# State-space phase and feed-forward opening of a hybrid layer: 108 named additions to VectorE, in a newly written order

## The chip, the cores and the metric

One core of a Trainium2 chip. The metric is the device time of one execution in microseconds (us). Engines: PE (TensorE, matrix products), DVE (VectorE), ACT (ScalarE), POOL (GpSimd) and SP, which here issues DMA transfers.

## The reference, cut to what matters

```python
xn = _rms_norm(h, pre_mix_norm); proj = xn @ w_in           # 2048 x 1024 tokens
y_ssd  = _ssd_mixer(...)      # state space: 16 chunks of 128 tokens, a running state, gate, norm
y_rwkv = _rwkv7_mixer(...)    # recurrent mixer
mix = concat([y_ssd, y_rwkv]) @ w_out
h  = h + _rms_norm(mix, post_mix_norm);  hn = _rms_norm(h, pre_ffn_norm)
u  = _causal_dwconv(hn @ ffn_w_up) ;  gate, val = split(u, 2)
y  = h + _rms_norm((silu(gate) * val) @ ffn_w_down, post_ffn_norm)
```

## The kernel before, in words

Three phases follow each other: `phase_R` (recurrent mixer, blocks R0 to R15), `phase_S` (state space, chunks C0 to C15 with shared work P0 to P7 for pairs of chunks, output projection and first residual), `phase_F` (feed-forward).

**Phase S.** A chunk n has these steps, each a list of small sub-steps that are numbered from 0. `z` is the gate projection; `decay` and `begin` make the decay matrix `Dt` and the inputs `Xdt`, `yt`; `off` (L1729) multiplies the old state into `of` and adds it to `yt` (sub-step 2, L1746); `y` (L1748) adds the products `py` (L1756, L1779), gates, squares and scales; `state` (L1783) first multiplies the old state `ST` by the chunk's decay (sub-step 0, L1794), then adds the new products (L1796); `o` is the output projection; `post` (L1849) does both norms, adds the input row (`m` plus `xi`, L1877), splits the result into two f16 halves (`hl` and, by L1862, the lower half in `xi`), turns both with DMA transposes into `tu` (L1867) and adds the turned halves into `hT` (`joined`, L1871: post.0/14 and post.1/4), which goes to DRAM (`HN`).

**Phase F** multiplies by a Strassen-like scheme of seven products. Blocks of `hn` (`hs`, loaded from `HN`) and of the weights (`us` from `w_up`, `r` from `w_down`) are added and subtracted (`ht`, `ut`, `rt`; L1946, L2098), then each is split into two f16 parts: ACT writes the upper part, DVE (L1976, L1978, L2329) the lower. The parts `w` are one buffer for each of the seven products; a part is stored to DRAM (`UW`) and read by the products `u` (L2125). DVE gathers the products in `C` (L2147), a convolution follows (L2182), then `p`, and its factors `fa` and `ft` (L1976, L2235).

**What sets the order.** From the end of phase R to the first 140 operations of phase F (the steps named E.0 and on) every step is built once in the order `TAIL`; then each engine's instructions are chained in the order in which their steps stand in the table `ORDER` (2325 names). So each engine, SP's DMA queue included, takes its work strictly in that order. After the table the planner `Program.run` orders phase F.

In phase F's entry and in `off`, `state` and `post` the two-operand additions without a PSUM operand are on POOL (`G_`) before.

Of the kernel before, what the change touches and what calls it, by code (L numbers as in the profile page):

```python
# [336 lines left out]
R14.solve/49 R15.low.1/0 R15.d.3/2 R13.finish.0/3 R15.low.1/1 R15.low.0/4 R14.solve/50 R14.solve/51 R14.solve/52
R14.conv.7/11 R14.solve/53 R15.low.1/2 R14.solve/54 R15.low.1/3 R14.solve/55 R13.finish.0/4 R15.d.5/0 R15.low.1/4
R13.finish.1/0 R15.d.5/1 R15.d.3/3 R15.d.3/4 R15.low.1/5 R15.scan/0 R14.solve/56 R14.solve/57 R13.finish.1/1
R14.values/0 R13.finish.1/2 R15.d.5/2 R15.low.1/6 R15.low.1/7 R14.solve/58 R13.finish.1/3 R14.solve/59 R14.solve/60  # L340
R15.d.6/0 R15.d.7/0 R14.solve/61 R15.low.1/8 R15.scan/1 R14.values/3 R13.finish.1/4 R15.low.1/9 R15.scan/3 R15.norm/4
R14.solve/62 R15.d.8/0 R15.d.5/3 R15.scan/4 R15.d.5/4 R14.values/1 R15.keys/0 R15.keys/1 R15.norm/0 R14.own.0/0
R14.solve/63 R15.norm/7 R15.d.7/1 R15.d.7/2 R14.solve/64 R14.solve/65 R14.solve/66 R15.norm/1 R15.scan/2 R15.d.9/0
R15.d.10/0 R15.norm/2 R14.solve/67 R14.solve/68 R14.solve/69 R15.norm/6 R14.solve/70 R14.solve/71 R15.d.9/1 R15.norm/5
R14.solve/72 R14.solve/74 R15.norm/8 R15.norm/12 R15.d.9/2 R15.d.7/3 R15.d.7/4 R15.norm/3 R14.values/4 R13.finish.1/5
R15.d.11/0 R15.d.9/3 R15.d.9/4 R15.d.12/0 R14.values/2 R15.norm/10 R15.receptance/0 R15.norm/11 R15.norm/9
R15.gram.0/0 R14.low.0/6 R14.solve/73 R14.solve/75 R15.receptance/2 R14.turn/0 R14.solve/76 R15.d.11/1 R14.conv.5/11
R14.turn/1 R14.merge.0/0 R15.gram.1/0 R15.gram.0/1 X.left/8 R14.own.0/1 R14.merge.0/1 R14.solve/77 R14.merge.0/2
R15.gram.0/2 R14.solve/78 X.left/7 R15.receptance/1 R15.gram.1/2 R14.own.0/2 R15.transposed.0/0 R15.gram.1/1
R14.merge.1/0 R13.finish.1/6 X.wdt/0 X.wz.0/0 R14.merge.1/1 R14.merge.1/2 R14.update.0/0 R14.update.0/1 R15.d.11/2  # L350
R15.transposed.0/1 X.wdt/1 X.wz.0/1 R15.solve/1 R15.d.13/0 R15.receptance/3 R15.receptance/4 X.wz.0/2 R13.finish.1/7
R15.d.13/1 R15.solve/0 R14.state.0/2 R15.solve/8 R15.d.11/3 R15.d.11/4 X.wdt/2 R15.solve/3 R13.finish.1/8
R14.state.0/5 R15.solve/2 R15.solve/7 R15.solve/5 R15.d.13/2 R15.solve/6 R15.solve/4 R15.conv.0/0 R14.own.1/0
R14.state.0/3 R14.state.1/0 P0.load.1/0 R15.conv.1/0 R14.state.0/4 R14.state.1/1 R13.finish.1/9 X.left/3 X.wz.1/0
R14.state.0/6 R15.solve/9 R15.conv.2/0 R15.solve/10 X.left/1 X.wz.0/3 R15.transposed.0/2 R14.own.1/1 R15.d.13/3
R15.conv.1/1 X.wz.0/4 X.wdt/3 R14.own.1/2 R15.d.13/4 R15.solve/11 R15.solve/12 R15.conv.1/2 X.left/2 R15.conv.3/0
R15.conv.1/3 R15.conv.1/4 X.left/5 R15.conv.3/1 R15.conv.3/2 R15.conv.1/5 P0.load.0/0 R14.update.1/0 X.wz.2/0
R15.conv.1/6 R15.conv.3/3 R15.transposed.1/0 R15.conv.3/4 R15.conv.1/7 R15.conv.3/5 R15.solve/13 R15.solve/14
R15.conv.3/6 R14.update.1/1 R15.solve/15 R15.solve/16 R15.solve/17 R15.solve/18 R15.solve/19 R15.solve/20 R15.solve/21
R15.solve/22 R15.solve/23 R15.solve/24 R15.solve/25 R15.solve/26 R15.solve/27 R15.solve/28 R15.solve/29 R15.solve/30  # L360
R15.solve/31 R14.state.1/5 R15.conv.3/7 R14.state.1/2 X.wz.1/3 R15.conv.1/8 R14.state.1/6 R14.gate/0 R15.conv.4/0
# [5 lines left out]
X.left/6 R15.solve/48 R15.solve/49 X.wz.2/4 R15.conv.5/3 X.wz.3/0 R15.solve/50 R15.solve/51 R15.conv.7/1 C0.z.1/0
R15.values/1 R15.conv.3/11 P1.load.0/0 R15.solve/52 R15.solve/53 R15.solve/54 R15.conv.5/4 R15.values/2 R15.conv.5/5
X.wz.3/1 R15.own.0/0 R15.values/3 X.wz.3/2 X.wz.3/3 C0.z.2/0 R15.conv.5/6 R15.solve/55 X.wz.3/4 C0.z.3/0
R14.finish.1/0 R15.own.0/1 C1.z.0/0 R15.conv.7/2 P0.steps/1 R15.solve/56 R15.solve/57 R15.solve/58 R15.solve/59  # L370
R15.solve/60 C1.z.1/0 C0.z.3/1 R15.conv.7/3 R15.conv.7/4 R15.solve/61 R15.solve/62 R15.conv.5/7 R15.conv.1/11 C0.z.3/2
R15.solve/63 R15.solve/64 P0.steps/2 R15.conv.7/5 X.wo.0/0 R15.conv.7/6 P0.steps/3 R15.conv.5/8 P1.load.1/0
R15.conv.5/9 P0.steps/4 R15.conv.7/7 C1.z.2/0 R15.low.0/5 X.wo.1/0 R15.solve/65 R15.conv.7/8 C0.begin/0 P0.steps/5
P0.steps/6 R15.conv.5/10 P0.sums/0 C0.begin/3 X.wo.0/1 X.wo.0/2 R15.solve/66 R15.solve/67 P0.sums/1 P0.flip/0
P0.flip/1 R15.solve/68 R15.solve/69 R15.solve/70 R15.solve/73 X.left/11 R15.solve/72 R15.solve/71 C0.z.3/3
R15.solve/74 R15.conv.7/9 R15.conv.7/10 C1.z.3/0 X.wo.1/1 X.left/9 X.wo.2/0 C1.z.3/1 R15.conv.5/11 X.wo.1/2 P1.steps/0
R15.solve/75 R15.solve/76 P0.flip/2 R15.conv.7/11 X.wo.3/0 P1.steps/1 C2.z.0/0 C2.z.1/0 C2.z.2/0 R15.solve/77
R15.values/4 R15.turn/0 R14.finish.1/1 R14.finish.1/2 R14.finish.1/3 R14.finish.1/4 P1.steps/2 R15.solve/78
R15.own.0/2 X.left/12 C1.z.3/2 X.wo.2/1 R15.turn/1 C0.rows/0 C1.z.3/3 R15.merge.0/0 R15.merge.0/1 C0.off/0
C0.decay.0/0 R15.merge.0/2 C0.decay.0/1 R15.merge.1/0 C0.decay.0/2 C0.decay.0/3 C2.z.3/0 C0.decay.1/0 C0.decay.0/4  # L380
P1.steps/3 R14.finish.1/5 C0.begin/1 R15.merge.1/1 C0.decay.0/6 C0.decay.0/7 R15.update.0/0 C2.z.3/1 C3.z.0/0
R14.finish.1/6 C0.decay.1/1 P2.load.0/0 X.wo.3/1 R15.update.0/1 C0.decay.1/2 C0.begin/2 C0.decay.1/3 X.wo.2/2
R15.state.0/0 C2.z.3/2 R15.state.0/5 R14.finish.1/7 C1.rows/0 R14.finish.1/8 R15.state.0/1 X.wo.4/0 X.wo.3/2
C0.decay.1/4 C0.decay.1/6 R15.merge.1/2 C3.z.1/0 X.wo.5/0 R15.state.0/2 C0.decay.1/8 C0.decay.0/5 X.wo.6/0 R15.own.1/0
R15.state.0/6 C3.z.2/0 P0.sums/2 C0.off/1 R15.state.0/3 X.wo.4/1 R15.state.0/4 C0.off/2 C0.decay.1/5 C0.decay.1/7
X.wo.4/2 R15.own.1/1 R15.own.1/2 C0.y/0 R15.update.1/0 X.wo.5/1 P1.steps/4 C0.y/1 R15.update.1/1 C0.y/2 C0.keys/0
# [2304 lines left out]
```

## Time and profile before

| | |
|---|---|
| median of 3 runs | 2531.79 us (2530.23 to 2536.94) |
| the profiled execution | 2531.92 us, span of its trace 2530.1 us |
| mean granted clock of TensorE | 0.983 of full speed |
| busy over the span | PE 95%, DVE 75%, POOL 48%, ACT 47% |

How it is read: busy times add up an engine's instructions, whatever waits for them. PEclk is the granted clock: 1.00 is 2.4 GHz and 0.5 is 1.2 GHz, so 0.93 over a stretch is a mix of both. The table ORDER covers about 798 to 1376 us of the span, of which 893 to 1246 us are mostly chunks.

### The profile page before, as it was taken

How to read it: one execution, taken by the hardware profiler on the slowest of the kernel's cores; microseconds unless marked ns; L12 is line 12 of the kernel's file. 1: busy time of each engine (PE TensorE's matmuls, PEld its weight loads, DVE VectorE, ACT ScalarE, POOL GpSimd, SP SyncE). 2: the span in 40 equal slices, each digit the busy share in tenths (PEclk: the TensorE clock that was granted, in tenths of full speed). 3: DMA queues.
4: the chain of work that ended last, by engine and by line, in shares of the span. 5: the costliest groups of instructions: out<-in, count | busy, mean ns of one | idle time of the engine just before them, and what ended most of it. 6: DMA issues, size and time to landing. Idle time of an engine off the chain costs nothing. (4 is left out here: it accounts for less than half of the span.)

```text
span 2530.1 us, 53854 instructions
## 1 busy us (share of the span) xinstructions
PE 2397.2 (95%) x21207; PEld 1516.7 (60%) x21212; DVE 1893.3 (75%) x3687; ACT 1198.0 (47%) x2407; POOL 1219.6 (48%) x1237
## 2 busy tenths in 40 slices
...
PEclk8899999999999999999999999999999999999999
...
GB/s 221 69 74 69 56 79 77 67 58 78 81 63 59 189 138 148 174 171 131 183 180 174 179 133 175 171 142 170 136 142 215 168 114 97 105 104 100 87 159 108
DMA packets 344413, 319.13 MB, mean 126 GB/s; under 512 B 203232, under 2 KB 248672, under 8 KB 340832
## 3 DMA queue, kind: packets, MB, share of 16 engines
...
q8 instruction: 166, 2.72, 0.4%
...
## 5 line engine op out<-in xcount | busy, mean ns | idle before, releaser
L2125 PE MATMUL u<-b,w 128*128 128x512 f16 x3696 | 811.0, 382 | 35.9 <-ACT C L2143 10.1
L2125 PEld LDWEIGHTS <-w 128*128 128x128 f16 x3696 | 363.1, 98 | 480.2 <-issue 40.3
L618 PE MATMUL d<-xt,wr 128*128 128x129 f16 x5376 | 333.8, 224 | 19.6 <-DMA xt<-xh 14.6
L618 PEld LDWEIGHTS <-wr 128*128 128x128 f16 x5376 | 320.2, 100 | 33.7 <-issue 15.9
L2365 PE MATMUL d<-dw,fa 128*128 128x512 f16 x1512 | 332.2, 379 | 5.2 <-DMA dw<-DW 2.9
L2365 PEld LDWEIGHTS <-fa 128*128 128x128 f16 x1596 | 156.4, 98 | 204.2 <-issue 16.1
L2147 DVE TENSOR_TENSOR C<-u,C 128x512 f32<-128x512 f32 x220 | 150.7, 685 | 159.8 <-PE u L2125 154.6
L618 PE MATMUL c<-xt,wc 128*128 128x131 f16 x3072 | 195.9, 224 | 11.0 <-ACT rc L846 4.8
L618 PEld LDWEIGHTS <-wc 128*128 128x128 f16 x3072 | 182.0, 98 | 17.5 <-issue 9.9
L2378 DVE TENSOR_TENSOR acc<-d,acc 128x512 f32<-128x512 f32 x212 | 140.3, 685 | 52.7 <-PE d L2365 51.8
L1976 POOL TENSOR_TENSOR fa<-p,fa 128x512 f16<-128x512 f32 x100 | 142.2, 1436 | 41.7 <-ACT fa L1971 41.7
L1978 DVE SCALAR_TENSOR_TENSOR w<-us,w 128x512 f16<-128x512 f32 x132 | 141.0, 1079 | 19.6 <-ACT w L1971 18.5
L2182 DVE SCALAR_TENSOR_TENSOR p<-C,fpar,p 128x1024 f32<-128x1024 f32 x88 | 127.5, 1449 | 34.5 <-ACT p L2178 34.5
L870 DVE SCALAR_TENSOR_TENSOR ca<-c,cw,ca 128x128 f32<-128x128 f32 x360 | 113.7, 345 | 29.9 <-ACT ca L860 25.8
L2182 DVE SCALAR_TENSOR_TENSOR a<-C,fpar,a 128x1024 f32<-128x1024 f32 x88 | 126.5, 1438 | 8.5 <-ACT a L2178 7.2
L1042 DVE TENSOR_TENSOR tmp<-atl,xl 128x60 f32<-128x60 f32 (+24 forms) x465 | 118.5, 255 | 16.4 <-DMA atl<-ATd 4.8
L2098 POOL TENSOR_TENSOR us<-us,us 128x512 f32<-128x512 f32 x66 | 109.2, 1657 | 44.6 <-DVE w L1978 23.5
L2143 ACT ACTIVATE C<-u 128x512 f32<-128x512 f32 x88 | 52.1, 592 | 162.1 <-PE u L2125 131.6
L1971 ACT ACTIVATE fa<-p 128x512 f16<-128x512 f32 x110 | 65.5, 623 | 125.2 <-DVE p L2195 113.4
L1971 ACT ACTIVATE w<-us 128x512 f16<-128x512 f32 x132 | 80.1, 623 | 91.5 <-POOL us L2098 29.3
L1048 DVE TENSOR_TENSOR xl<-xl,tmp 128x60 f32<-128x60 f32 (+24 forms) x465 | 112.3, 242 | 14.5
L2188 POOL COPY fcarry<-C 128x2 f32<-128x2 f32 x88 | 38.1, 434 | 161.6 <-DVE C L2147 161.6
...
## 6 DMA issues: line engine op xcount, KB each, us to landing
...
```

What stands on the lines that cost most here:

```text
L618: nc.tensor.matmul(ps, w[:, a, kt, :], xt[:, b, kt, cols], start=n == 0, stop=n == 3 * KT - 1)
L870: V.scalar_tensor_tensor(out=acc[:, q], in0=m["rc", e][:, q, k:k + 128], scalar=cw[:, e + q, k:k + 1], in1=acc[:, q], op0=ALU.mult, op1=AL ...
L1042: chain.tensor_tensor(out=self.tmp[:, :k, :n], in0=self.atl[:, j, j + 1:32].unsqueeze(1).to_broadcast([P, k, n]), in1=self.xl[:, :k, j:j + ...
L1048: chain.tensor_tensor(out=self.xl[:, :k, j + 1:32], in0=self.xl[:, :k, j + 1:32], in1=self.tmp[:, :k, :n], op=ALU.add)
L1971: S.activation(h, src, AF.Copy, **({} if scale is None else {"scale": scale}))
L1976: {"V": V, "G": G_}[engine].tensor_tensor(out=l, in0=src, in1=h, op=ALU.subtract)
L1978: V.scalar_tensor_tensor(out=l, in0=src, scalar=scale, in1=h, op0=ALU.mult, op1=ALU.subtract)
L2125: nc.tensor.matmul(bk[at], self.w[i][:, u, k, :], self.half.b[i][:, k, v, :], start=start and n == 0, stop=n == 11, skip_group_check=True)
L2147: op("V", .61, lambda: V.tensor_tensor(out=part(j, x), in0=bk[at], in1=part(*a), op=ALU.add), (("u", 4 * s + at), (*(c0, c1)[a[0]], a[1])) ...
L2182: V.scalar_tensor_tensor(out=o[j], in0=C[j][:, 2 - d:1026 - d], scalar=cw(g, 2 - d), in1=o[j], op0=ALU.mult, op1=ALU.add)
L2365: nc.tensor.matmul(bk[s, t], pairs[m].a[i][:, u, t * P:t * P + P], pairs[m].w[n][0][:, v, :], start=new and m == 0 and u == v == 0, stop=m ...
L2378: V.tensor_tensor(out=acc[j][:, t], in0=bk[s, t], in1=acc[j][:, t], op=ALU.add)
```

## The change

A set `SWAP` of 108 step names is added. While a step is built, `Steps.now` holds its name, and `either(G_, V)` gives DVE for a step in `SWAP`, POOL for every other. The additions of `off`, `state`, `post` and of phase F's `add`, `sub`, `plus` go through `either`. The table `ORDER` is written anew for all engines, with the same 2325 names.

```diff
+def either(pool, vector):
+    return vector if Steps.now in SWAP else pool
...
 def note(name, step):
...
+    Steps.now = name
     tc = Steps.made["tc"]
     n = len(traced(tc))
     step()
     Steps.made[name] = list(traced(tc)[n:])
+    Steps.now = None
...
 ORDER = """
-R14.conv.7/9 R13.state.1/3 R15.d.0/0 R13.state.1/4 R14.conv.7/10 R13.state.1/6 R13.finish.0/0 R14.d.13/1 R15.d.1/0
...
+SWAP = frozenset("""
+C0.off/2 C0.state/0 C1.off/2 C1.state/0 C2.off/2 C0.post.0/14 C2.state/0 C3.off/2 C1.post.0/14 C1.post.1/4 C3.state/0
...
+""".split())
...
-                products, scaled, lambda: G_.tensor_tensor(out=self.yt, in0=self.yt, in1=self.t, op=ALU.add)]
+                products, scaled, lambda: either(G_, V).tensor_tensor(out=self.yt, in0=self.yt, in1=self.t, op=ALU.add)]
...
-                lambda: G_.tensor_tensor(
+                lambda: either(G_, V).tensor_tensor(
                     out=s1, in0=s0, in1=self.aend.unsqueeze(2).to_broadcast([P, 8, 64]), op=ALU.mult),
...
-                G_.tensor_tensor(out=self.hT, in0=self.tu[:, 0], in1=self.tu[:, 1], op=ALU.add)
+                either(G_, V).tensor_tensor(out=self.hT, in0=self.tu[:, 0], in1=self.tu[:, 1], op=ALU.add)
...
         def sub(out_, a, b):
-            G_.tensor_tensor(out=out_, in0=a, in1=b, op=ALU.subtract)
+            either(G_, V).tensor_tensor(out=out_, in0=a, in1=b, op=ALU.subtract)
...
-                    op("G", 1.25, lambda: G_.tensor_tensor(out=st[o], in0=st[a], in1=st[b], op=alu), (n[a], n[b]), (n[o],))
+                    op("G", 1.25, lambda: either(G_, V).tensor_tensor(out=st[o], in0=st[a], in1=st[b], op=alu), (n[a], n[b]), (n[o],))
```

The same edit is made in `add`, in the plus of `factors` (L2235) and in the addition of L1877, of which no step is in `SWAP`.

Counted in the built programs, 103 instructions go from POOL to DVE: 16 of `off` (L1746), 13 of `state` (L1794), 27 of `post` (L1871), 29 of L1946, 15 of L2098 and 3 of L2235. The other five names in `SWAP` (E.306, E.310, E.313, E.317, E.319) are the lower halves of `fa`, whose function has no `either`: they stay on POOL. In the new order 35 of the 103 stand before the products `py` of chunk 10, 11 more before those of chunk 12, and 57 behind them. Lines of the changed kernel are 17 higher from `phase_R` on (L1746 is L1763 there).

**Place 1: chunk 13 joins its state while chunk 11 is finished.** POOL before; `hT_110` is chunk 11's first joined half, `ST0` the state, `sgr` a norm's factor, `hs` and `ht` blocks of the feed-forward input.

```order
L1746 TENSOR_TENSOR yt_13_20555<-yt_13_20555,of_13_20570 128x512
L1608 TENSOR_SCALAR pnv_20683<-ssh_11_20681 128x1
L1612 TENSOR_TENSOR pnr_20685<-pnv_20683,mhalf_s_17704 128x1
L1794 TENSOR_TENSOR ST0_17025<-ST1_17026,aend_13_20584 128x512
L1946 TENSOR_TENSOR hs00310_21480<-hs00310_21480,hs00300_21476 128x512
L1871 TENSOR_TENSOR hT_110_20693<-tu_110_20690 128x512
L1608 TENSOR_SCALAR sgv_20719<-sgs_13_20715 128x2
L1946 TENSOR_TENSOR ht003_21487<-hs00311_21482,hs00310_21480 128x512
L1612 TENSOR_TENSOR sgr_20721<-sgv_20719,mhalf_s_17704 128x2
```

DVE with the change, the same place; the first row makes the lower half that the transposes turn for chunk 11's second half.

```order
L1879 TENSOR_TENSOR xi_11_20367<-xi_11_20367,hl_11_20672 128x512
L1993 TENSOR_TENSOR b2_0_21429<-hs00210_21460,b2_0_21429 128x512
L1993 TENSOR_TENSOR b0_0_21420<-hs00300_21476,b0_0_21420 128x512
L1658 SCALAR_TENSOR_TENSOR sz_13_20612<-th_13_20614,sz_13_20612 128x512
L1888 TENSOR_TENSOR hT_110_20693<-tu_110_20690 128x512
L1811 TENSOR_TENSOR ST0_17025<-ST1_17026,aend_13_20584 128x512
L1796 TENSOR_TENSOR yt_13_20555<-py_13_20704,yt_13_20555 128x512
L1813 TENSOR_TENSOR ST0_17025<-pst_13_20750,ST0_17025 128x512
L1797 TENSOR_TENSOR yt_13_20555<-yt_13_20555,sz_13_20612 128x512
```

The joined half, which waits for a DMA, and the state's multiply now stand in DVE's queue, ahead of chunk 13's `yt` and state.

**Place 2: the third weight block of the opening.** POOL before: the differences `ut`, `us` of weight block 3 between the down-projection's `r` and the factors `fa` of block pair 0.

```order
L1946 TENSOR_TENSOR ut_0_3_22119<-us_0_300_22078,us_0_310_22053 128x512
L2098 TENSOR_TENSOR us_0_310_22053<-us_0_310_22053,us_0_311_22102 128x512
L2098 TENSOR_TENSOR us_0_300_22078<-us_0_310_22053,us_0_300_22078 128x512
L1946 TENSOR_TENSOR r_0_0_21791<-rt_0_0_21792,r_0_0_21791 128x512
L1946 TENSOR_TENSOR r_0_1_22056<-r_0_1_22056 128x512
L1946 TENSOR_TENSOR rt_0_1_22057<-r_0_1_22056 128x512
L1976 TENSOR_TENSOR fa4_0_0_21960<-p_0_1_21933,fa4_0_0_21960 128x512
L2235 TENSOR_TENSOR ft_0_0_21949<-p_0_1_21933,p_0_0_21710 128x512
```

DVE with the change, the same weight block.

```order
L1963 TENSOR_TENSOR ut_0_3_22119<-us_0_300_22078,us_0_310_22053 128x512
L2164 TENSOR_TENSOR C_0_21_22074<-u_0_21_22060,C_0_20_22073 128x512
L2164 TENSOR_TENSOR C_0_21_22074<-u_0_22_22081,C_0_21_22074 128x512
L1879 TENSOR_TENSOR xi_15_21180<-xi_15_21180,hl_15_21269 128x512
L1995 SCALAR_TENSOR_TENSOR w5_0_2_21884<-us_0_201_21857,w5_0_2_21884 128x512
L2199 SCALAR_TENSOR_TENSOR a_0_1_21939<-C_0_11_21808,fpar_21405,a_0_1_21939 128x1024
L2115 TENSOR_TENSOR us_0_310_22053<-us_0_310_22053,us_0_311_22102 128x512
L2212 TENSOR_TENSOR p_0_1_21933<-p_0_1_21933,a_0_1_21939 128x1024
L2115 TENSOR_TENSOR us_0_300_22078<-us_0_310_22053,us_0_300_22078 128x512
L2252 TENSOR_TENSOR p_0_0_21710<-p_0_0_21710,p_0_1_21933 128x512
```

The weight differences now alternate on DVE with the gathering of products, the convolution and the splits; POOL keeps the `fa` halves and the small copies.

## Rows read from the trace of the kernel before

**Rows 1.** The page: busy time, share and instructions of engines, and the granted clock in 40 slices of the span.

```profile
PE 2397.2 (95%) x21207; PEld 1516.7 (60%) x21212; DVE 1893.3 (75%) x3687; ACT 1198.0 (47%) x2407; POOL 1219.6 (48%) x1237
...
PEclk8899999999999999999999999999999999999999
```

**Rows 2.** Busy time of each engine in five windows that cover the table ORDER (from:to and length, busy us and instructions of each engine; then the granted clock, the DMA share and GB/s).

```profile
core 0: us, PE busy (x) PEld busy (x) DVE busy (x) ACT busy (x) POOL busy (x), PEclk, DMA share, GB/s
798.00:893.00 95.00, 91.81 (x1313) 74.40 (x1310) 69.09 (x190) 55.38 (x124) 50.15 (x96) 1.00 0.46 143
893.00:1112.00 219.00, 215.37 (x1299) 125.14 (x1302) 142.34 (x305) 97.83 (x277) 95.75 (x107) 0.99 0.53 145
1112.00:1168.00 56.00, 52.50 (x301) 29.50 (x300) 38.15 (x74) 26.09 (x68) 31.00 (x31) 1.00 0.80 214
1168.00:1246.00 78.00, 63.62 (x304) 34.10 (x305) 59.24 (x92) 37.19 (x98) 46.40 (x45) 0.89 0.46 127
1246.00:1374.00 128.00, 104.21 (x460) 45.89 (x460) 100.46 (x98) 56.59 (x94) 100.36 (x80) 0.93 0.64 199
```

**Rows 3.** What PE waited for, 1168 to 1374 us (total, times, longest).

```profile
PE u L2125 <- ACT w L1971: 9.5, 1, 9.5
PE u L2125 <- DVE C L2147: 5.8, 4, 2.9
PE u L2125 <- DVE b L1976: 4.3, 1, 4.3
PE pst L1789 <- DVE Xd L1718: 3.3, 1, 3.3
```

**Rows 4.** One line that does the same kind of addition on both engines, over the whole span (durations in ns: min/median/max; first and last start).

```profile
L2235 DVE TENSOR_TENSOR p<-p,p x22: 677/691/1632, 1329.7 to 2470.4; 128x512 f32<-128x512 f32 x22
...
L2235 POOL TENSOR_TENSOR ft<-p,p x22: 1257/1266/1732, 1338.0 to 2473.7; 128x512 f32<-128x512 f32 x22
```

**Rows 5.** POOL's groups, 1168 to 1374 us (count, busy us, mean ns of one, idle before and its releasers): five of which most instructions move, and two (L1877, L1976) that stay.

```profile
L2098 POOL TENSOR_TENSOR us<-us,us 128x512 f32<-128x512 f32 x16 | 27.1, 1695 | 5.2 <-ACT C L2143 1.9 <-DVE w L1978 1.5 <-DMA us<-in_w_u_dram 1.3
L1871 POOL TENSOR_TENSOR hT<-tu 128x512 f32<-128x512 f16 x12 | 15.4, 1286 | 8.9 <-DMA tu<-xi 7.4 <-issue 1.4
L1877 POOL TENSOR_TENSOR m<-m,xi 128x1024 f32<-128x1024 f32 x5 | 12.7, 2530 | 5.8 <-DVE m L1875 4.2 <-DMA xi<-in_x_dram 1.5
L1946 POOL TENSOR_TENSOR ut<-us,us 128x512 f32<-128x512 f32 x6 | 9.5, 1575 | 0.0
L1976 POOL TENSOR_TENSOR fa<-p,fa 128x512 f16<-128x512 f32 x5 | 8.1, 1625 | 1.6 <-ACT fa L1971 1.6
L1946 POOL TENSOR_TENSOR hs<-hs,ht 128x512 f32<-128x512 f32 x4 | 7.7, 1932 | 0.6 <-POOL pnr L1612 0.3
...
L1746 POOL TENSOR_TENSOR yt<-yt,of 128x512 f32<-128x512 f32 x4 | 5.1, 1270 | 0.0
```

**Rows 6.** DVE's costliest groups, 1168 to 1374 us, shapes kept apart, in the same columns.

```profile
L1978 DVE SCALAR_TENSOR_TENSOR w<-us,w 128x512 f16<-128x512 f32 x28 | 26.9, 969 | 12.6 <-ACT w L1971 12.6
L1976 DVE TENSOR_TENSOR b<-hs,b 128x512 f16<-128x512 f32 x19 | 19.1, 1014 | 5.5 <-ACT b L1971 5.5
L2147 DVE TENSOR_TENSOR C<-u,C 128x512 f32<-128x512 f32 x20 | 13.7, 684 | 3.6 <-PE u L2125 3.2
L2182 DVE SCALAR_TENSOR_TENSOR p<-C,fpar,p 128x1024 f32<-128x1024 f32 x8 | 12.5, 1567 | 1.0 <-ACT p L2178 1.0
L2182 DVE SCALAR_TENSOR_TENSOR a<-C,fpar,a 128x1024 f32<-128x1024 f32 x7 | 11.8, 1679 | 4.8 <-ACT a L2178 4.7
L1862 DVE TENSOR_TENSOR xi<-xi,hl 128x512 f16<-128x512 f32 x10 | 9.7, 968 | 0.2 <-ACT hl L1885 0.2
L1875 DVE SCALAR_TENSOR_TENSOR m<-m,por,gpost 128x1024 f32<-128x1024 f32 x5 | 9.3, 1857 | 5.0 <-POOL por L1612 5.0
```

**Rows 7.** Durations of two of these lines in that window (ns: min/median/max).

```profile
L1978 DVE SCALAR_TENSOR_TENSOR w<-us,w x28: 678/693/1758, 1214.8 to 1361.7; 128x512 f16<-128x512 f32 x28
...
L2182 DVE SCALAR_TENSOR_TENSOR p<-C,fpar,p x8: 1272/1282/2294, 1285.5 to 1367.3; 128x1024 f32<-128x1024 f32 x8
```

**Rows 8.** What DVE waited for, 1168 to 1374 us (total, times, longest).

```profile
DVE w L1978 <- ACT w L1971: 12.6, 8, 2.9
DVE b L1976 <- ACT b L1971: 5.5, 5, 2.3
DVE m L1875 <- POOL por L1612: 5.0, 4, 3.0
DVE a L2182 <- ACT a L2178: 4.7, 3, 3.5
DVE yt L1779 <- POOL yt L1746: 4.1, 1, 4.1
DVE yt L1768 <- POOL sgr L1612: 3.4, 1, 3.4
```

**Rows 9.** What ACT waited for, 1168 to 1374 us (total, times, longest).

```profile
ACT w L1971 <- DMA UW<-w: 17.7, 3, 7.1
ACT w L1971 <- issue: 10.6, 3, 5.5
ACT C L2143 <- DVE p L2182: 10.4, 3, 5.4
```

**Rows 10.** The turned halves `tu` over the whole span: who waited for them, and the time from the issue of their DMA to its landing.

```profile
  POOL hT L1871: 34.4, 9
...
DMA to landing us min/median/max: 2.4/2.8/7.3
```

More of the change, by code (lines that the diff above doesn't have):

```diff
@@ L183, in note @@
     Steps.made[name] = list(traced(tc)[n:])
+    Steps.now = None
 class Steps:
-    made, kind = None, ""
+    made, now, kind = None, None, ""
     def do(self, name, *a, only=None):
@@ L337 @@
[L337 to L361, printed above, removed]
@@ L367 @@
[L367 to L386, printed above, removed]
@@ new lines @@
+R15.receptance/0 R15.d.12/0 R15.gram.0/0 R15.receptance/2 R14.values/2 R14.turn/0 R14.turn/1 R14.merge.0/0
+R15.gram.0/2 R15.d.11/1 R15.gram.1/0 R15.transposed.0/0 R13.finish.1/6 X.wz.0/0 R14.merge.0/1 R14.merge.0/2
+R15.gram.0/1 X.wdt/1 R14.merge.1/0 X.wdt/2 R15.gram.1/2 R14.own.0/2 R15.solve/0 R14.merge.1/1 R14.merge.1/2 X.left/2
+R15.solve/1 R15.gram.1/1 R14.update.0/0 X.wdt/3 R15.d.13/0 R15.d.11/2 R15.d.11/3 R14.update.0/1 R13.finish.1/7
+R13.finish.1/8 R15.solve/2 R14.state.0/2 R15.d.11/4 R14.state.0/5 R15.solve/3 X.left/3 R15.d.13/1 X.left/8 X.wz.0/3
@@ new lines @@
+R14.finish.1/6 R15.conv.7/10 X.left/11 P0.flip/2 R15.own.0/2 C0.z.3/3 R15.solve/75 R15.solve/76 C2.z.1/0 C0.rows/0
+R15.conv.7/11 R15.turn/1 C2.z.2/0 C2.z.3/0 R15.turn/0 R15.merge.0/0 X.wo.2/1 R15.conv.5/11 C0.decay.0/0 R15.solve/77
+C1.z.3/2 R15.state.0/0 R15.merge.0/1 R15.merge.0/2 C0.begin/1 X.left/12 R15.solve/78 X.wo.3/0 R15.merge.1/0
+R15.state.0/1 C0.decay.0/1 R15.merge.1/1 C0.decay.0/2 C0.off/0 C2.z.3/1 C0.decay.0/3 C0.decay.0/4 R15.update.0/0
+C3.z.0/0 C0.begin/2 X.wo.3/1 X.wo.2/2 C0.decay.0/6 C0.decay.0/7 R15.update.0/1 X.wo.3/2 C0.off/1 C0.decay.1/0
@@ new lines @@
+C0.decay.1/1 R15.state.0/2 X.wo.4/0 C0.decay.1/2 C0.decay.1/3 R15.state.0/3 X.wo.5/0 C0.decay.1/4 R15.state.0/5
+R15.state.0/4 R14.finish.1/7 C0.decay.0/5 C0.decay.1/5 R15.merge.1/2 C3.z.1/0 R15.own.1/0 R15.own.1/1 C0.decay.1/6
+R15.state.0/6 C0.decay.1/8 C0.decay.1/9 C1.begin/3 C0.keys/0 C1.rows/0 R15.own.1/2 P2.load.0/0 C0.decay.1/7 C0.y/0
+X.wo.5/1 C1.decay.0/0 X.wo.4/1 R15.update.1/0 X.wo.6/0 X.wo.5/2 R15.state.1/0 C1.decay.0/1 R15.update.1/1 C0.off/2
+C1.decay.0/2 C1.decay.0/3 C1.decay.0/4 C0.keys/1 C0.y/1 C3.z.2/0 C0.y/2 R15.state.1/5 R14.finish.1/8 C0.state/0 C0.y/4
```

383 lines of the change are left out of this document (211 added, 172 removed).

## The prediction, made before the changed kernel ran

> **What bounds the kernel now.** I read the page first, then the windows of the stretch that the new table orders, then the waits of PE, DVE and ACT in the worst of them, and last the durations of the operations that move.
>
> PE is busy 95% of the span [rows 1], so the change can give back only what PE loses inside its own stretch. The windows [rows 2] show where that is. From 798 to 893 us PE lacks 3.2 us, from 893 to 1112 us 3.6 us, from 1112 to 1168 us 3.5 us. From 1168 to 1374 us, the last chunks and the feed-forward opening, it lacks 38.2 us of 206 (78.0 minus 63.6 and 128.0 minus 104.2), and the granted clock there is 0.89 and 0.93, a mix of both levels. Call these stretches one to four. Only the fourth holds much.
>
> In stretch four no engine is full: DVE is busy 159.7 us of 206 and POOL 146.8 [rows 2]. PE waits in turn for weights that ACT and DVE split, for the gathering of products and for a block of the input [rows 3]: a chain that runs through POOL's differences, ACT's upper halves, DVE's lower halves, and back. So latency and DVE's queue decide there, not one engine's sum.
>
> **What a moved operation costs.** One line does the same addition on both engines [rows 4]: alone it takes 0.68 us on DVE (median 0.69) and 1.26 us on POOL. In stretch four the moved groups take POOL 1.27 to 1.93 us each [rows 5]. 103 instructions move, not 108: five of the names belong to a function that has no choice of engine. The five that stay leave 5 x 0.69 = 3.5 us less on DVE.
>
> **What they do to each other.** The gathering L2147, with a PSUM operand, takes 0.684 us in the busiest part of the stretch, but the splits L1978 and L1976, which read two SBUF tiles, take 0.969 and 1.014 us on the mean [rows 6], against a minimum of 0.678 us and a median of 0.693 us for L1978 [rows 7]. For 1024 columns the alone time is 1.28 us, the means 1.57, 1.68 and 1.86 us [rows 6, 7]. Over the six SBUF groups shown that is 28 x 0.28 + 19 x 0.33 + 8 x 0.29 + 7 x 0.40 + 10 x 0.28 + 5 x 0.58 = 25 us in which DVE is stretched beside POOL; smaller groups of this kind may add a third, so I take 33 us. The Trainium skill's page SBUF — State Buffer, section Who interferes with whom, explains it: an instruction with two SBUF inputs on VectorE and one of GpSimd that reads SBUF share a read interface as an exclusive lock. By that rule each moved operation holds the interface 0.69 us in place of 1.27, and the stretching goes down with it; the trace agrees as far as the PSUM-fed row goes.
>
> **The sum, stretch four.** 57 of the moved instructions stand there. POOL loses 57 at about 1.5 us, some 87 us of its 146.8. DVE gains 57 x 0.69 = 39.3 us: 159.7 + 39.3 = 199.0. POOL's load falls to 41%, so of 33 us of stretching about 19 go; the moved operations themselves, two SBUF inputs each, meet what POOL still does, at about 0.13 us each (0.33 us a piece now, times 41%): 7.5 us. DVE ends at 199.0 - 19 + 7.5 = 187 us of work. Bounds: 166 us if all stretching goes (199.0 - 33), 199 if none does. I take 187, by POOL's remaining share.
>
> DVE now waits 46 us in this stretch. Of that 12.5 us are for POOL (por, yt, sgr) and 22.8 for ACT (w, b, a) [rows 8]. The POOL part shrinks, since what stays on POOL is small and no longer queues behind 1.27 us additions; the ACT part stays as long as ACT itself waits 17.7 us for the stores of w to land [rows 9], which nothing here changes. But waiting time fills with the 27 us of added work. I take 8 us of waits that remain exposed: 187 + 8 = 195 against 206, **11 us gained**. PE's work, 167.8 us as it stands, fits below.
>
> **Stretches one to three.** In the third DVE goes from 38.2 to 38.2 + 11 x 0.69 = 45.8 of 56 us, and PE keeps the bound at 52.5: I take 2 of its 3.5 us. The first two are at PE's end but for 6.8 us; DVE has 26 and 77 us free there, and 35 x 0.69 = 24 us come. I take 2 us of these 6.8.
>
> **The joined halves.** 27 of the moved additions wait for a DMA. On POOL that cost 34.4 us of waiting [rows 10] and nobody's time. On DVE the same wait stops the queue: at place 1 a joined half stands in front of the state and of chunk 13's yt. The transposes land 2.4 to 7.3 us after their issue [rows 10]; in the new order DVE has mostly 4 to 6 us of other work, some six to nine instructions of 0.69 us, between a chunk's first lower half and its sum, so I expect waits of 0 to 3 us on 14 first halves. Lower bound 0, upper bound 14 x 3 = 42 us, nearly all in stretch two, where DVE has 77 us free; within stretch four at most 3 x 3 = 9 us. They are inside the 8 us above. The new order also moves SP's issues; they keep their predecessors, and I cost that at nothing, covered by the 0.46 to 0.80 DMA share [rows 2]; if that cover is gone, it is the second rival.
>
> Sum: 11 + 2 + 2 = **15 us**. The profiled execution took 2531.9 us, equal within 0.2 to the median of the runs, so I forecast 2531.9 - 15 = **2517 us**. Behind 1374 us I change nothing.
>
> **Rivals.**
> 1. *DVE becomes the bound of the opening, and the kernel is slower.* Place: stretch four. If the stretching stays as it is and DVE's 22.8 us of waits for ACT do not fill, DVE needs 199.0 + 22.8 = 222 us, 16 more than now; with 4 gained before, 2544. It decides from the point where DVE's work and its unfilled waits pass 206 us. For it: weights, gathering, convolution and splits now stand in one queue (place 2), each behind an instruction with a wait of its own. Against it: POOL's load more than halves.
> 2. *Nothing comes back.* The longest PE wait, 9.5 us [rows 3], is for an upper half on ACT, which waits 17.7 us for stores of w and 10.6 us for no profiled reason [rows 9]. If these stores and the DMA queue set the pace, stretch four stays 206 us and the time is 2531.9 - 4 = 2528, no change that can be measured. The Trainium skill's Perfetto Trace Analysis, section Optimizing Scalar/DVE Operations, leads to the same number by another way: GPSIMD and DVE share a read port, so moving work between the two might not help. Rows 4 speak against that reason, since the same addition holds its engine 0.69 in place of 1.27 us.
> 3. *PE sets the pace throughout.* All stretching goes (166 us of DVE work), stretch four falls to PE's 168 us and all 10.3 us of the others come back: 2531.9 - 38.2 - 10.3 = 2483.
> 4. *The change does less than it says*: 103 of 108 move, which I have counted.
>
> **How the numbers follow.** About 0.3%, 7.6 us, is what a measurement of this kernel can tell from no change, so faster is below 2524, slower above 2539. Forecast 0.57 (its own range 2500 to 2524); rival 3 0.06; rival 2 0.20; rival 1 0.17. Faster 0.57 + 0.06 = 0.63, same 0.20, slower 0.17. The low end, 2500, is DVE's lower bound with some waits (166 + 11 = 177 us in stretch four, 29 gained, and 3 elsewhere); the high end, 2540, takes in rival 2 and the near part of rival 1. Outside lie rival 3 and most of rival 1, about 0.2.
>
> **What would show it.** In the changed profile the windows of stretch four should be about 11 us shorter, with DVE at 90% or more and POOL under 40%; L1978's and L1976's means should fall from about 1.0 to about 0.8 us; POOL's hT row should all but vanish and a wait of DVE for tu appear, of a few us in all. The forecast is wrong if the means do not fall (rival 1), if ACT's wait for the stores of w grows as the gaps shrink (rival 2), or if PE's gap in stretch four closes (rival 3).

## The result and the profile after

The changed kernel takes **2508.0 us** (median of 4 runs, 2506.5 to 2510.2), the kernel before 2531.5 in the same session: a ratio of 0.9904, 95% interval 0.9887 to 0.9921. The forecast was 2517 in a range of 2500 to 2540. The span of the profiled execution is 2504.7 us against 2530.1. The rows of the changed kernel below have its own line numbers: L1995, L1993 and L1888 are L1978, L1976 and L1871 of before.

The page, the same lines as [rows 1]:

```profile
PE 2396.9 (96%) x21212; PEld 1519.2 (61%) x21212; DVE 1911.8 (76%) x3790; ACT 1197.9 (48%) x2407; POOL 1079.8 (43%) x1134
...
PEclk8899999999999999999999999999999999999999
```

103 instructions went from POOL to DVE (1237 to 1134, 3687 to 3790). POOL lost 140 us of work and DVE gained only 18.5, a quarter of 103 x 0.69 = 71: the rest of DVE's work became shorter.

The windows of the changed kernel, columns as in [rows 2]; stretch four, 1168 to 1374 us before, now ends at 1351:

```profile
core 0: us, PE busy (x) PEld busy (x) DVE busy (x) ACT busy (x) POOL busy (x), PEclk, DMA share, GB/s
798.00:893.00 95.00, 89.57 (x1251) 72.01 (x1250) 65.41 (x180) 52.07 (x117) 46.90 (x93) 0.96 0.46 145
893.00:1112.00 219.00, 214.87 (x1305) 124.35 (x1304) 156.28 (x342) 99.16 (x280) 56.53 (x73) 1.00 0.53 146
1112.00:1168.00 56.00, 53.85 (x314) 29.74 (x313) 43.98 (x87) 27.07 (x73) 19.83 (x23) 1.00 0.63 180
1168.00:1351.00 183.00, 163.93 (x810) 81.01 (x807) 165.46 (x254) 95.90 (x194) 61.90 (x72) 0.98 0.68 202
```

The gain is in the fourth: 206 to 183 us, 23 of the 25.4 us by which the two spans differ (the other 2.4 us lie behind it). What PE lacks there halves, from 38.2 to 19.1 us; it is busy 3.9 us less, at a granted clock of 0.98 in place of 0.92 over the stretch. DVE's 165.5 us are 90% of the stretch, POOL's 61.9 are 34%. The first three gain nothing: chunk 12's products begin at 1168.5 us (1166.7 before).

DVE's groups in 1168 to 1351 us, which answer to [rows 6], with two that moved (L2115, L1888):

```profile
L1995 DVE SCALAR_TENSOR_TENSOR w<-us,w 128x512 f16<-128x512 f32 x28 | 20.6, 746 | 0.0
L1993 DVE TENSOR_TENSOR b<-hs,b 128x512 f16<-128x512 f32 x20 | 13.5, 680 | 0.0
L2115 DVE TENSOR_TENSOR us<-us,us 128x512 f32<-128x512 f32 x15 | 12.2, 816 | 0.0
L2199 DVE SCALAR_TENSOR_TENSOR a<-C,fpar,a 128x1024 f32<-128x1024 f32 x8 | 11.1, 1388 | 0.0
L2199 DVE SCALAR_TENSOR_TENSOR p<-C,fpar,p 128x1024 f32<-128x1024 f32 x8 | 10.2, 1276 | 0.2 <-ACT p L2195 0.2
L1879 DVE TENSOR_TENSOR xi<-xi,hl 128x512 f16<-128x512 f32 x10 | 7.8, 779 | 0.1
...
L1892 DVE SCALAR_TENSOR_TENSOR m<-m,por,gpost 128x1024 f32<-128x1024 f32 x5 | 6.4, 1283 | 1.6 <-POOL por L1629 1.6
L1888 DVE TENSOR_TENSOR hT<-tu 128x512 f32<-128x512 f16 x9 | 6.1, 683 | 0.7 <-DMA HN<-hT 0.7
```

L1993 falls from 1.014 to 0.680 us, L1995 from 0.969 to 0.746, m from 1.857 to 1.283: nearly back to what they take alone. The waits of ACT in 1168 to 1351 us, which answer to [rows 9] (total, times, longest):

```profile
ACT hl L1875 <- POOL m L1894: 8.1, 5, 3.8
...
ACT w L1988 <- issue: 6.6, 2, 5.7
...
ACT w L1988 <- DMA UW<-w: 5.0, 2, 3.4
...
ACT C L2160 <- POOL fcarry L2205: 2.5, 1, 2.5
```

The wait for the stores of w fell from 17.7 to 5.0 us. It did not only change its name: all of ACT's waits before a part w fell from 38.5 us there to 24.8. PE's waits there, which answer to [rows 3]:

```profile
PE u L2142 <- ACT C L2160: 6.6, 2, 4.7
PE u L2142 <- DVE C L2164: 6.2, 3, 3.7
PE u L2142 <- DVE b L1993: 3.9, 2, 3.6
```

The 9.5 us for the upper half of w are gone; the gathering of products C is what PE waits for now. The joined halves, the answer to [rows 10], over the span (who waited for tu):

```profile
  DVE hT L1888: 7.6, 3
```

### The profile page after: what moved, and what is told of

Same layout as the page of the kernel before. It is cut to its first block, busy times and chain, and to the rows that moved or that the text cites. A ratio compares the mean times of both kernels' runs of the same rounds, so it can differ in the third digit from the quotient of the medians.

```text
span 2504.7 us, 53819 instructions
## 1 busy us (share of the span) xinstructions
PE 2396.9 (96%) x21212; PEld 1519.2 (61%) x21212; DVE 1911.8 (76%) x3790; ACT 1197.9 (48%) x2407; POOL 1079.8 (43%) x1134
## 5 line engine op out<-in xcount | busy, mean ns | idle before, releaser
L2142 PE MATMUL u<-b,w 128*128 128x512 f16 x3696 | 808.5, 381 | 24.5 <-ACT C L2160 11.5
L2382 PEld LDWEIGHTS <-fa 128*128 128x128 f16 x1596 | 157.1, 98 | 204.7 <-issue 18.3
L1993 POOL TENSOR_TENSOR fa<-p,fa 128x512 f16<-128x512 f32 x100 | 140.7, 1421 | 50.7 <-ACT fa L1988 50.7
L1995 DVE SCALAR_TENSOR_TENSOR w<-us,w 128x512 f16<-128x512 f32 x132 | 133.1, 1020 | 7.0 <-ACT w L1988 5.9
L1988 ACT ACTIVATE fa<-p 128x512 f16<-128x512 f32 x110 | 65.4, 623 | 124.6 <-DVE p L2212 112.7
L1988 ACT ACTIVATE w<-us 128x512 f16<-128x512 f32 x132 | 80.2, 624 | 85.0 <-POOL us L2115 29.1
L2115 POOL TENSOR_TENSOR us<-us,us 128x512 f32<-128x512 f32 x51 | 83.9, 1648 | 45.8 <-DVE w L1995 27.3
```

What stands on the lines that cost most here:

```text
L1988: S.activation(h, src, AF.Copy, **({} if scale is None else {"scale": scale}))
L1993: {"V": V, "G": G_}[engine].tensor_tensor(out=l, in0=src, in1=h, op=ALU.subtract)
L1995: V.scalar_tensor_tensor(out=l, in0=src, scalar=scale, in1=h, op0=ALU.mult, op1=ALU.subtract)
L2142: nc.tensor.matmul(bk[at], self.w[i][:, u, k, :], self.half.b[i][:, k, v, :], start=start and n == 0, stop=n == 11, skip_group_check=True)
L2382: nc.tensor.matmul(bk[s, t], pairs[m].a[i][:, u, t * P:t * P + P], pairs[m].w[n][0][:, v, :], start=new and m == 0 and u == v == 0, stop=m ...
```

## The experiments

Ratios are to the kernel before on the same chip. Two lengths from each trace are compared throughout: from the first product `py` of chunk 0 to the first of chunk 12 (**chunks**), and from there to the start of the 384th product `u`, the end of the opening (**opening**). The start of chunk 0 itself lies between 891 and 903 us in these profiles, without a pattern that an edit would explain, so single profiles are good to some us, and verdicts rest on the timed medians. The edits to `SWAP` change the kernel's length, so lines shift by some between the runs (ACT's L1988 is L1978 in e1); the names of the tiles say which instruction is meant.

| run | time, us | ratio, 95% interval | chunks | opening |
|---|---|---|---|---|
| before | 2531.5 | 1 | 274.8 | 205.4 |
| changed | 2508.0 | 0.9904 (0.9887 to 0.9921) | 272.9 | 181.8 |
| e1 new order, nothing moved | 2547.3 | 1.0052 (1.0035 to 1.0069) | 285.1 | 203.3 |
| e2 old order, all moved | 2548.6 | 1.0051 (1.0031 to 1.0071) | 291.6 | 207.1 |
| e3 new order, names E moved | 2524.3 | 0.9951 (0.9935 to 0.9967) | 289.9 | 184.8 |
| e4 new order, names C moved | 2529.5 | 0.9984 (0.9971 to 0.9997) | 272.9 | 196.3 |
| e5 changed, POOL reads in vain | 2564.3 | 1.0110 (1.0083 to 1.0137) | 276.1 | 227.4 |
| e6 changed, halves back | 2522.6 | 0.9958 (0.9943 to 0.9973) | 284.3 | 184.3 |
| e7 late part alone | 2504.8 | 0.9891 (0.9876 to 0.9906) | 273.6 | 182.1 |
| e8 early part alone | 2538.8 | 1.0024 (1.0013 to 1.0035) | 279.4 | 204.7 |
| e9 changed, POOL writes in vain | 2563.1 | 1.0118 (1.0103 to 1.0133) | 277.7 | 231.0 |
| e10 e7 and m + xi moved | 2507.5 | 0.9894 (0.9877 to 0.9910) | 273.4 | 186.5 |
| e11 as e5, fewer | 2534.3 | 1.0006 (0.9991 to 1.0021) | 277.8 | 204.6 |
| e12 as e9, fewer | 2523.4 | 0.9953 (0.9934 to 0.9971) | 274.9 | 196.8 |

**Order and engine apart.** e1 keeps the new order and moves nothing; e2 moves all in the order of before.

```diff
-SWAP = frozenset("""
...
+SWAP = frozenset("""""".split())
```

> The new order with an empty SWAP: all 103 additions back on POOL. Theory (the engine makes the gain: an addition holds POOL 1.27 to 1.9 us and stretches DVE's two-SBUF instructions beside it): the gain of 23.5 us goes, and since the new order was written for short additions the time is at or above the kernel before, 2530 to 2550 us; the means of L1995 and L1993 in the opening are back near 1.0 us. Rival (the new written order makes the gain): 2508 to 2515 us.

```diff
 ORDER = """
-R14.conv.7/9 R13.state.1/6 R14.conv.7/10 R13.state.1/3 R14.conv.7/11 R14.solve/35 R15.d.0/0 R13.finish.0/0
...
+R14.conv.7/9 R13.state.1/3 R15.d.0/0 R13.state.1/4 R14.conv.7/10 R13.state.1/6 R13.finish.0/0 R14.d.13/1 R15.d.1/0
...
```

> The change's SWAP with the order of the kernel before. Theory: most of the stretching of DVE goes as well, so a good part of the gain stays, 2512 to 2522 us. Rival (order): 2530 us or more. A third reading, in which swap and order only work together because additions in DVE's queue at the old places wait for transposes and loads: above 2532 us, with DVE waits for tu and hs of over 20 us.

Each alone is 0.5% slower than before; together they gain 1%. e1 is in the range of its theory, e2 in that of its third reading, but DVE's waits for tu and hs in e2, 18 us from 798 to 1391 us, are under the 20 that this reading asked for. The window of the opening in e2, in the columns of the windows above:

```profile
1183.00:1391.00 208.00, 169.39 (x774) 80.91 (x774) 170.45 (x249) 93.75 (x193) 62.45 (x69) 0.93 0.57 170
```

ACT's longest wait there:

```profile
ACT w L1988 <- DMA UW<-w: 17.3, 3, 7.0
```

PE's two longest:

```profile
PE u L2142 <- DVE C L2164: 10.1, 5, 2.8
PE u L2142 <- ACT w L1988: 8.5, 1, 8.5
```

POOL is as light as in the changed kernel, and DVE with all the moved additions has 170 us of work, where by the forecast's sum it would have 199.0 unrelieved. Yet the stretch keeps its 207: ACT still waits for the stores of w, PE for ACT. Relief of DVE and a light POOL buy nothing there by themselves. As PE waits longer still, in five pieces, for DVE's gathering, the stores of w are one cause of it, and not shown to be the only one. In e1 that wait is 0.8 us, so the new order takes it away; whether it does so by ACT's places, DVE's or those of SP's stores wasn't separated. But in e1 POOL's queue steps in. Its window of the opening:

```profile
1182.00:1386.00 204.00, 170.84 (x778) 82.18 (x777) 167.50 (x194) 94.24 (x191) 142.80 (x124) 0.92 0.61 181
```

ACT's waits in it:

```profile
ACT hl L1865 <- POOL m L1884: 13.7, 5, 5.5
ACT C L2150 <- POOL fcarry L2195: 9.3, 1, 9.3
...
ACT b L1978 <- POOL hs L1953: 7.7, 2, 5.1
ACT w L1978 <- POOL us L2105: 7.6, 5, 2.6
...
ACT w L1978 <- DMA UW<-w: 0.8, 1, 0.8
```

The first four are 38.3 us. A copy of 128x2 elements (fcarry) keeps ACT waiting 9.3 us because it stands behind POOL's additions, which run without a gap before it; in the changed kernel it is 2.5. The kernel before has no such wait although its POOL is as full (146.8 us of 206): the place in the queue counts, and not only the load. In its chunks e2 loses 17 us; why wasn't isolated.

**The names apart.** Both in the new order.

```diff
 SWAP = frozenset("""
-C0.off/2 C0.state/0 C1.off/2 C1.state/0 C2.off/2 C0.post.0/14 C2.state/0 C3.off/2 C1.post.0/14 C1.post.1/4 C3.state/0
...
```

> The change with only the E names of SWAP (47 additions of the feed-forward opening on DVE, the 56 of the chunks back on POOL). Theory (the gain sits behind chunk 12, where most moved additions are those of the opening): 2509 to 2516 us. Rival (the chunks' additions carry it, since they stand in the state's and the output's chain): 2522 us or more.

e4 is the counterpart, without the names E.

> The change with only the C names of SWAP (56 additions of the chunks on DVE, the 47 of the opening back on POOL). Theory (gain in the opening): 2522 to 2535 us, with L1995 near 0.95 us on the mean. Rival (chunks carry it): 2509 to 2516 us.

The times fall in the range of e3's rival and of e4's theory, and the gain stands whole in neither. The two halves are each other's complement: e3 has the opening (184.8) and loses 15 us in the chunks, e4 has the chunks (272.9, as the changed kernel) and 9 of the 24 us in the opening. With the opening's additions on POOL, PE waits up to 11.7 us for the gathered C and ACT for fcarry, in e4 from 1169 to 1366 us:

```profile
ACT C L2152 <- POOL fcarry L2197: 9.3, 1, 9.3
```

**The joined halves** go back to POOL in e6.

```diff
 SWAP = frozenset("""
-C0.off/2 C0.state/0 C1.off/2 C1.state/0 C2.off/2 C0.post.0/14 C2.state/0 C3.off/2 C1.post.0/14 C1.post.1/4 C3.state/0
...
+C0.off/2 C0.state/0 C1.off/2 C1.state/0 C2.off/2 C2.state/0 C3.off/2 C3.state/0 C4.off/2 C4.state/0 C5.off/2 C5.state/0
...
```

> The changed kernel with the 27 joined halves (the sums of hT, each behind the landing of a transpose) back on POOL; everything else as changed, the same written order. DVE loses 27 x 0.69 = 18.6 us of work, nearly all in stretches one and two, where PE has 95% and more, and the 7.6 us for which it waited for tu. Theory A (the joined halves neither gain nor cost: the gain stands in the opening): 2508 within 4. Rival B (their waits in DVE's queue ate the gain forecast for stretches one to three): 2500 to 2504, 4 to 8 faster than changed. Rival C (what comes after waits for the halves, and POOL's 1.26 us and later turn hold up the chunks): 2512 to 2520.

14 us slower than changed: rival C, 3 us above its range. Of the 17 us by which e3's chunks are longer than the changed kernel's, 11 come with the halves alone (284.3 against 272.9). POOL's longest wait in e6, 898 to 1184 us:

```profile
POOL hT L1880 <- DMA tu<-xi: 60.5, 9, 10.3
```

DVE's waits there for POOL:

```profile
DVE xi L1889 <- POOL pnr L1621: 12.4, 9, 2.7
DVE m L1884 <- POOL por L1621: 10.4, 8, 3.9
DVE yt L1777 <- POOL sgr L1621: 8.1, 5, 2.1
```

Where a half waits for its transposes, the factors of the norms (pnr, por, sgr) wait behind it: DVE is held up 30.9 us. In the changed kernel, 893 to 1168 us, it is 12.1:

```profile
DVE yt L1785 <- POOL sgr L1629: 4.5, 3, 2.0
DVE xi L1897 <- POOL pnr L1629: 4.2, 6, 1.0
DVE m L1892 <- POOL por L1629: 3.4, 7, 0.9
```

**Early and late part.** e7 takes the order of before up to `C11.y/0` and then the remaining names as the new order has them, with the 68 names of SWAP that fall there; e8 the reverse, with the other 40.

```diff
...
 SWAP = frozenset("""
-C0.off/2 C0.state/0 C1.off/2 C1.state/0 C2.off/2 C0.post.0/14 C2.state/0 C3.off/2 C1.post.0/14 C1.post.1/4 C3.state/0
...
+C9.post.0/14 C9.post.1/4 C11.state/0 C12.off/2 C10.post.0/14 C13.off/2 C11.post.0/14 C11.post.1/4 C13.state/0
...
```

> The order of before up to C11.y/0 (about 1110 us of the span), then the new order for what remains, and 68 of the additions on DVE, those that are issued in that remainder. Theory A (order and engine change need each other only in the late chunks and the opening, where DVE's queue is nearly full): 2508 within 4, all of the gain. Rival B (the new order of the early chunks prepares the later ones, as less POOL work is left over by chunk 11): half of the gain or less, 2516 to 2526. Rival C (nothing comes back unless all is changed): 2528 or more.

> The counterpart: the new order up to C11.y/0, then the order of before, with the 40 additions of the first part on DVE and the rest on POOL. Theory A (the early part gains nothing): 2531 within 5. Rival B (the early part prepares the later): 2515 to 2525. If the old order of the late part no longer fits what the new early part leaves behind, 2536 to 2545.

The late part has all of the gain (theory A); the early part gains nothing and by its ratio costs some 6 us, which is the last case of its expectation. In e8 the wait of ACT for the stores of w is back, 1172 to 1379 us:

```profile
ACT w L1962 <- DMA UW<-w: 17.9, 3, 7.4
```

Whether e7 is faster than the changed kernel itself stays open: the intervals overlap.

**Useless work on POOL.** Is the gain of the opening that DVE is no longer stretched, or that POOL's queue is short? e5 and e11 give POOL additions that read SBUF, e9 and e12 instructions that only write it, at each of the 63 names of `SWAP` in chunks 12 to 15 and the opening; no engine but POOL depends on them. First e5, against the changed kernel:

```diff
...
+            Steps.idle = wk.tile([P, 10, 16], F16, name="idle"), wk.tile([P, 16], F32, name="idle1")
+            G_.memset(Steps.idle[1], 0.0)
...
+    for name in ORDER.split():
+        if name in SWAP and name.split(".")[0] in ("E", "C12", "C13", "C14", "C15"):
+            n = len(traced(tc))
+            some = Steps.idle[1].unsqueeze(1).to_broadcast([P, 10, 16])
+            for _ in range(3):
+                tc.nc.gpsimd.tensor_tensor(out=Steps.idle[0], in0=some, in1=some, op=ALU.add)
+            Steps.made[name] += list(traced(tc)[n:])
```

> The changed kernel, with useless work given back to POOL: after each of the 63 swapped steps of chunks 12 to 15 and of the opening POOL adds a small SBUF tile (128x160) three times, on a tile that nobody else reads. No engine waits for it but POOL itself; by POOL's other rows I estimate 0.4 to 0.5 us for each, 80 us in all, about what the moved additions took there. Theory A (the gain of the opening comes from taking POOL's SBUF work away, so that DVE's two-operand instructions are not stretched): L1995's mean goes back up from 0.746 toward 0.95 us, stretch four grows by 8 to 20 us, and the time is 2516 to 2528. Rival B (the gain is only the shorter way through the queues: 0.69 for 1.27 us, and no hand-over between engines): 2508 within 4, with L1995's mean below 0.80.

e9, against e5, repeats a fill of 128x192 in its place, eight times a step:

```diff
...
-            for _ in range(3):
-                tc.nc.gpsimd.tensor_tensor(out=Steps.idle[0], in0=some, in1=some, op=ALU.add)
+            for _ in range(8):
+                tc.nc.gpsimd.memset(Steps.idle[0], 0.0)
```

> As the run in which POOL repeated useless additions at the 63 swapped steps of chunks 12 to 15 and of the opening, but with instructions that only write: at each step POOL fills a small SBUF tile (128x192) eight times, by POOL's own MEMSET rows (0.52 us for 512 columns, 0.11 for 8) an estimated 0.26 us each, 2.1 us a step, as much of POOL's time as the additions took (2.2 us a step). What lies in POOL's queue behind them, the small instructions of the normalisations, is as late as there. Theory A (the stretching comes from SBUF reads of POOL beside DVE's two-operand ones): L1995's w stays at 0.75 to 0.80 us, and what is left of the 56 us over the changed kernel is the queue's share: 2515 to 2540. Rival B (any work of POOL stretches DVE, or the queue alone makes the 56 us): w at 0.85 us or more, or the time 2555 or more. Rival C (the queue costs nothing and the reads everything): 2508 within 5.

2564 and 2563, slower than before: e5 is far above both its theories, and e9 is what its rival B forecast for the queue alone, 2555 or more, while w stayed at 0.78 us as its theory A had it. My price for an addition was too low (0.736 us on the mean, not 0.45), so POOL was overfull, 185.3 and 175.5 us of 228. The window of the opening in e5:

```profile
1179.00:1407.00 228.00, 173.61 (x783) 81.55 (x781) 194.15 (x253) 94.12 (x194) 185.33 (x248) 0.91 0.55 163
```

and in e9:

```profile
1179.00:1407.00 228.00, 173.72 (x758) 80.65 (x757) 162.95 (x249) 93.03 (x190) 175.52 (x537) 0.87 0.54 161
```

DVE's waits for POOL in that window of e9:

```profile
DVE xi L1897 <- POOL pnr L1629: 10.5, 4, 6.7
DVE m L1892 <- POOL por L1629: 10.3, 3, 3.7
```

ACT's wait there for POOL's carry copy:

```profile
ACT C L2161 <- POOL fcarry L2206: 20.1, 2, 18.1
```

In e5 the same DVE instructions take 194.2 us, in e9 163.0, and the time is the same. With the writes beside it DVE isn't stretched more than in the changed kernel (165.5), so what is lost in e9 is lost behind POOL's queue. DVE waits 20.8 us for the factors of the norms, ACT 20.1 us for the carry copy. The fills themselves are untouched too (0.251 to 0.318 us), while the additions of 160 columns spread from 0.445 to 1.504. The Trainium skill, SBUF — State Buffer, section Who interferes with whom, states just this: a DVE instruction with two SBUF inputs contends with a GpSimd instruction that reads SBUF, not with one that only writes it. The runs agree (194.2 against 163.0 us of DVE work).

For the size that the kernel before had, e11 gives two additions a step and e12 five fills:

```diff
-            for _ in range(3):
+            for _ in range(2):
```

> The changed kernel with two useless additions on POOL at each of the 63 swapped steps of chunks 12 to 15 and of the opening, in place of three: by the 0.70 to 0.78 us that one took there, 1.4 to 1.5 us a step, about what a moved addition took on POOL before (1.27 to 1.93), so that POOL's load is that of the kernel before, some 145 us in stretch four, while the additions themselves stay on DVE. Theory A (the stretching of DVE is what the change took away in the opening): 2518 to 2530, L1995's w at 0.85 us or more. Rival B (POOL's queue is: the small instructions of the normalisations and the carry copies come late): 2518 to 2535 as well, and the run with writes alone agrees with it within 5. Rival C (POOL's queue costs only when it is overfull, and the stretching only takes time that DVE has): 2512 or less.

```diff
-            for _ in range(8):
+            for _ in range(5):
```

> The same load on POOL as writes alone: five fills of 128x192, 0.258 us each, 1.3 us a step. Theory A (stretching): 2508 to 2514, w at 0.78 us or less. Rival B (POOL's queue): within 5 of the run with additions, 2518 to 2535, with waits of DVE for por and pnr of over 10 us and of ACT for the carry copy. Rival C: 2512 or less, and so the run with additions.

The window of the opening in e11:

```profile
1178.00:1383.00 205.00, 168.53 (x779) 80.28 (x779) 186.67 (x252) 94.21 (x192) 152.64 (x189) 0.94 0.63 181
```

DVE's row of w in it:

```profile
L1997 DVE SCALAR_TENSOR_TENSOR w<-us,w 128x512 f16<-128x512 f32 x28 | 22.8, 824 | 0.0
```

ACT's wait for the carry copy in it:

```profile
ACT C L2162 <- POOL fcarry L2207: 11.6, 2, 8.7
```

The same three views of e12, first the window:

```profile
1168.00:1365.00 197.00, 167.30 (x779) 80.58 (x779) 168.35 (x252) 94.60 (x193) 133.60 (x368) 0.93 0.64 188
```

DVE's row of w:

```profile
L1996 DVE SCALAR_TENSOR_TENSOR w<-us,w 128x512 f16<-128x512 f32 x28 | 19.7, 714 | 0.0
```

ACT's wait for the carry copy:

```profile
ACT C L2161 <- POOL fcarry L2206: 12.7, 2, 10.3
```

With POOL filled up to 152.6 us (146.8 before) by work that reads, the whole gain is gone, 2534.3; with writes, 133.6 us, 15 of these 26 us are (12 by the ratios). DVE's work is 186.7 in the one and 168.4 in the other. So most of what the changed kernel loses here is lost behind POOL's queue, and at most some 11 us (13 by the ratios) to the stretching of DVE; as e12 fills POOL 19 us less than e11, some of these may be queue too. None of the three theories as written came true whole: A missed both times (2534 and 2523) and e11's w, 0.824 us, B asked for two equal runs, C for no loss.

The traces of the other runs point the same way. In the new order the opening grows with POOL's work in its window: 182 to 187 us in the five runs with 51 to 81 us of it (changed, e3, e6, e7, e10), 196.3 with 125.0 (e4), 196.8 with 133.6 (e12), 203.3 with 142.8 (e1), 204.6 with 152.6 (e11), and 227 to 231 with 185.3 and 175.5 (e5, e9). It does not follow DVE's work: that is 165.5 us in the changed kernel, 167.5 in e1 and 186.7 in e11, and e1 and e11 differ by 1.3 us. In the order of before the opening is 205 to 207 us with 62.5 us of POOL's work (e2) as with 146.8. Different instructions fill POOL in these runs, so this is a comparison and not a test, but it leaves the stretching little of the opening's gain.

**One step further.** e10 moves four more additions in e7.

```diff
+ C12.post.0/4 C13.post.0/4 C14.post.0/4 C15.post.0/4
```

> The late part alone (2504.8), and four more additions on DVE: m + xi of chunks 12 to 15, 1024 columns, 2.43 us on POOL and by DVE's rows of 1024 columns 1.28. They stand in the chain that ends in the next normalisation (m, m + xi, pnr, xi), for which DVE waits 3.8 us in stretch four. Theory A (DVE is now the bound of the opening, 166 us of 183): 4 x 1.28 = 5 us more, 2508 to 2512. Rival B (the chain is: 1.15 us and a hand-over shorter each time): 2498 to 2502. Rival C (neither): 2505 within 3.

2507.5, an interval that overlaps e7's: no difference can be told, so A and C stay both; B, the shorter chain, is out. Moving these four to DVE pays nothing.

## Why the prediction was right, and where its steps were not

- **Place.** Right: 23 us come back in stretch four, and e7 shows that changing the late part alone brings all of the gain.
- **The price of a moved addition.** Right: 0.683 us for hT, 0.816 for us, and 0.751 on the mean of the 57 in stretch four, 42.8 us, against 0.69 and 0.13 for the meetings. POOL lost 84.9 us there, 87 forecast.
- **Relief of the stretching, 19 less 7.5 us.** Mis-sized. DVE's work came to 165.5 us, the forecast's lower bound (166), not 187: by 199.0 - 165.5, 33.5 us went in place of 11.5. Without the moved additions DVE's work fell from 159.7 to 165.5 - 42.8 = 122.7 us, for 190 instructions and then 197: 37 us went, more than the 33 that I took for all the stretching. I had scaled it with POOL's whole load; if only POOL's additions of two operands count, 39.4 of its 61.9 us (127.1 of 146.8 before, sums of the rows of 512 columns and more), 33 x (1 - 39.4 / 127.1) = 23 us would have gone, which explains a part. And that this relief is what shortens the stretch was the forecast's path, which the runs do not bear out: in e2 DVE has 170.5 us of work and the stretch keeps its length.
- **"the ACT part stays as long as ACT itself waits 17.7 us for the stores of w to land [rows 9], which nothing here changes."** This step failed. The new order does change it: 5.0 us in the changed kernel, 4.5 in e4, 0.8 in e1; with the order of before it stays (17.3 in e2, 17.9 in e8). I read the diff as a move between engines and took the order as a carrier. It was the other half of the gain.
- **8 us of exposed waits.** Too small: DVE idles 17.5 us in stretch four, 46 before. 165.5 + 17.5 are the 183 us measured, where the forecast had 187 + 8 = 195: the work was put 21.5 us too high and the waits 9.5 too low. 23 us gained there in place of 11.
- **Stretches one to three, 4 us.** Wrong: nothing came. DVE waits 7.6 us for tu and 17.3 for the state's products in 798 to 1168 us in place of other waits, and e8 shows no gain from the early part by itself.
- **The joined halves on DVE.** Right in size: 7.6 us in three waits, all before 1168 us, against a bound of 42. That on POOL they were "nobody's time" is wrong for the new order (e6, 14 us). For the order of before no run moves them alone; there too DVE waits 24.5 us for pnr, sgr and por from 893 to 1168 us.
- **Rivals.** The second, that nothing comes back since ACT's wait for the stores sets the pace, is what the move alone does in the opening (e2). The Trainium skill's Perfetto Trace Analysis, section Optimizing Scalar/DVE Operations, which holds that moving work between GPSIMD and DVE might not help, agrees with e2's time, though not by the shared port that it gives as the reason (DVE's work there is 170.5 us and not 199.0), and not with the change as a whole. The first did not come: DVE's work and waits are 183 us, not 222. The third came halfway: DVE's work is at its 166 us, but PE's gap did not close.

The forecast was 9 us too high, and that it was no further off is in part luck: 21.5 us too much work, 9.5 us too few waits and 4 us promised where nothing came cancel down to 8. Nor does its path hold. It had DVE's relief shorten the stretch with ACT's wait for the stores unchanged; where that wait stays, in e2, the relief comes and the stretch is as long as before. The move and the order together shortened POOL's queue and took the wait away, and the forecast had costed what the new order does to SP's issues at nothing. None of the three signs of being wrong that it named appeared: only the run without the order (e2) shows the failed step.
